# Encoder step: the convolution in three stretches instead of five, the sample's inputs in one tile with the last prompt inputs

## The chip, the core and the metric

The kernel runs on one core of one Trainium2 chip. The metric is the device time of one execution in microseconds (us). The kernel before takes 1810.93 us, the median of 3 runs (1809.39 to 1812.55). About 0.2% is what a measurement of this kernel can tell from no change.

## What is computed

One step of a streaming encoder of depth 1, for a prompt of 1024 tokens and a sample of 64 tokens that share the weights; both are kept side by side as 1088 columns. After a norm, one projection feeds four mixers: a convolution module, forgetting attention (fox), a gated recurrence (hgrn) and stick-breaking attention (sb), 256 channels each. Their outputs go through `w_out`; then come memory cross-attention, a squared-ReLU MLP and a final norm. The change touches the convolution module, here with the end of the layer that uses it:

```python
def _conv_module(a, g, hist, w, bias, ln_g, ln_b):
    u = a * sigmoid(g)
    ext = concatenate([hist, u], axis=1)         # hist: 30 rows before the first token
    y = depthwise_conv(ext, w)                   # 31 taps per channel
    yf = y + bias
    yn = layer_norm(yf, ln_g, ln_b)              # over the 256 channels
    return silu(yn), ext[:, -30:]
...
    x = x + concat([conv_o, fox_o, hg_o, sb_o]) @ w_out
```

The prompt's `hist` is zero, the sample's is the input `cache_conv`. The last 30 rows of `ext` of each are outputs (`conv_p`, `conv_s`).

## The kernel before, in words

**Layout.** Channels lie on the 128 partitions, tokens along the free dimension, columns 0 to 1023 the prompt, 1024 to 1087 the sample. Matrix products are made of three float32 passes (high and low parts): each weight tile of 512 KB is fetched on SP's queue (L179, tile `wr`, two buffers), copied to its high part on ACT (`wh`, L74) and subtracted to its low part on DVE (`wl`, L171), each with two buffers.

**Lanes.** The mixers are written as four generators that a loop (L980) advances by a virtual time: projections (`lane_projections`), attention, convolution and hgrn. What a generator yields is its estimate of the time of the piece just recorded. Every lane has a priority; the framework's scheduler then orders the instructions of each engine by priority and readiness. Projections come first, then attention, hgrn and convolution, and products on TensorE (`products`) behind these. The last thing the projection lane does is `memory_kv` (L371): 16 weight tiles of `w_mk` and `w_mv` ("the kv tiles"); each ends with a copy `mkvT` and a copy `mnat` on ACT. After the lanes, with a still later priority (PR_END), comes the rest.

**The convolution** (`lane_conv`, L740) works on stretches of the sequence: 288, 288, 288 and 160 columns of the prompt, then the 64 of the sample. For a stretch and each of the two channel halves it reads the value and gate projections back from DRAM (`ga`, `gg`, L756 and L757), makes the sigmoid on ACT and DVE, writes the product into `ext` (L759) behind the 30 columns of history, and runs 31 taps on DVE, each one instruction over the whole stretch (L764 for the first, L767 for thirty). Then comes the layer norm over channels, which lie on partitions: two sums on TensorE through a matrix of ones (`pme`, `pva`), the square root's reciprocal by `rstd_chain` (L140), scale and shift, another sigmoid, and a store to `mix_d` in DRAM (L799). Tiles with one buffer each, shared by tag: `c0`, `c1`, `c2` (288 columns; inputs, gates, and the norm's three work tiles), `ce0`, `ce1` (318; `ext`, then the squares), `cy0`, `cy1` (288; the results `y`).

**After the lanes** `mix_d` is read back: for columns 0 to 511 ("group 0", tile `mix`, L1000), and for 512 to 1087 ("group 1", tile `aq`, L1000 through `split_mix` at L1186). Each tile is split into high and low parts (`ap`). `dense_add` (L1072) multiplies by `w_out`: eight weight tiles for group 0 (tile `pa`, 512 columns), then eight for group 1 (320 and 256 columns), and adds each product to the residual `xt` (L1083), which L1159 loads. Group 1 multiplies slots 2 to 7 of the mixers first and the convolution's slots 0 and 1 last (`MIX`, L1189). Between the groups, `rms_stats` and `rms_apply` (L1041, L1063) make the norm of group 0: squares (L1038), a sum `pr` on TensorE, eight normed tiles (L1059) and their splits. Memory attention follows with `pq`.

Of the kernel before, what the change touches and what calls it, by code (L numbers as in the profile page):

```python
# [8 lines left out]
F32 = mybir.dt.float32  # L9
# [3 lines left out]
AF = mybir.ActivationFunctionType  # L13
# [4 lines left out]
P = 128  # L18
# [34 lines left out]
def kernel(ctx: ExitStack, tc: tile.TileContext, *args):  # L53
# [666 lines left out]

    HW = CW - 1
    CN = 288

    def ct_(name, tag, n=CN):
        return hc.tile([P, n], F32, name=name, tag=tag)
# [14 lines left out]
    def lane_conv():  # L740
        tails = [None, None]
        for t0, n in [(t, min(CN, SP - t)) for t in range(0, SP, CN)] + [(SP, SS)]:
            last = t0 + n >= SP
            ys, exts = [], []
            for ct in range(2):
                yield Need(ct)
                yield Need(2 + ct)
                ext = ct_(f"ext{ct}", f"ce{ct}", CN + HW)
                if t0 == SP:
                    V.tensor_copy(out=ext[:, :HW], in_=hT[:, ct])  # L750
                elif t0 == 0:
                    V.memset(ext[:, :HW], 0.0)
                else:
                    V.tensor_copy(out=ext[:, :HW], in_=tails[ct])
                ga, gg, sg = ct_("ga", "c0"), ct_("gg", "c1"), ct_("sg", "c2")
                nc.sync.dma_start(out=ga[:, :n], in_=pj_d[ct][:, t0:t0 + n])  # L756
                nc.sync.dma_start(out=gg[:, :n], in_=pj_d[2 + ct][:, t0:t0 + n])  # L757
                sigmoid(sg[:, :n], gg[:, :n])
                V.tensor_tensor(out=ext[:, HW:HW + n], in0=ga[:, :n], in1=sg[:, :n], op=ALU.mult)  # L759
                if not last:  # L760
# [5 lines left out]
                for j in range(1, CW):  # L766
                    V.scalar_tensor_tensor(out=y[:, :n], in0=ext[:, j:j + n], scalar=cwT[:, ct, j:j + 1], in1=y[:, :n],  # L767
                                           op0=ALU.mult, op1=ALU.add)
                    if j % 6 == 5:
                        yield 0.3 + n / 130.0  # L770
                ys.append(y[:, :n])
                exts.append(ext)
            if last:
                ps = ps_cv.tile([P, G], F32, name="pco", tag="cv")
                for ct in range(2):
                    nc.tensor.transpose(ps[:HW, ct * P:(ct + 1) * P], exts[ct][:, n:n + HW], ident)
                ot = ct_("cvo", "c0")
                V.tensor_copy(out=ot[:HW, :G], in_=ps[:HW])
                nc.sync.dma_start(out=(conv_s if t0 == SP else conv_p)[0, 0], in_=ot[:HW, :G])
            pm = ps_cv.tile([P, 512], F32, name="pme", tag="cv")  # L780
            for ct in range(2):
                mm(pm[:, :n], ones, ys[ct], ct == 0, ct == 1)
            sq = [ct_(f"sq{ct}", f"ce{ct}", CN + HW)[:, :n] for ct in range(2)]
            for ct in range(2):
                V.scalar_tensor_tensor(out=ys[ct], in0=pm[:, :n], scalar=-1.0 / G, in1=ys[ct],
                                       op0=ALU.mult, op1=ALU.add)
                act(sq[ct], ys[ct], AF.Square)
            pv2 = ps_cv.tile([P, 512], F32, name="pva", tag="cv")
            for ct in range(2):
                mm(pv2[:, :n], ones, sq[ct], ct == 0, ct == 1)  # L790
            r = rstd_chain(hc, n, pv2[:, :n], ("c0", "c1", "c2"), scale=1.0 / G)
            for ct in range(2):
                V.tensor_tensor(out=ys[ct], in0=ys[ct], in1=r, op=ALU.mult)
                V.tensor_scalar(out=ys[ct], in0=ys[ct], scalar1=cvec[:, 1, ct:ct + 1], scalar2=cvec[:, 2, ct:ct + 1],
                                op0=ALU.mult, op1=ALU.add)
                sg = ct_("sg2", "c2")[:, :n]
                sigmoid(sg, ys[ct])
                V.tensor_tensor(out=ys[ct], in0=ys[ct], in1=sg, op=ALU.mult)
                nc.sync.dma_start(out=mix_d[ct][:, t0:t0 + n], in_=ys[ct])  # L799
                yield 0.5 + n / 150.0  # L800
# [688 lines left out]
```

## Time and profile before

| | |
|---|---|
| median of 3 runs | 1810.93 us (1809.39 to 1812.55) |
| the profiled execution | 1812.65 us |
| its span, first to last instruction | 1810.6 us |
| busy in the span: PE, DVE, ACT, POOL | 96%, 66%, 44%, 5% |
| mean granted TensorE clock | 0.982 of 2.4 GHz |
| last kv product ends, first `pa` starts | 671.2 and 673.6 us |
| `w_out` group 0, first `pa` to last add | 673.6 to 729.6 us |
| `w_out` group 1, to its last product | 729.6 to 791.2 us |

The engines are PE (TensorE), DVE (VectorE), ACT (ScalarE), POOL (GpSimd) and SP, which issues nearly all transfers. Every engine runs its own instructions in the order in which they stand. A busy PE is not necessarily a PE at its full rate, so its time is read from a stage's length beside the rate of an undisturbed tile. PEclk is the granted clock as a share of 2.4 GHz.

### The profile page before, as it was taken

The page shows a single profiled execution, that of the slowest core. Times are in us where ns is not written, and L with a number is a line of the kernel's source. Part 1 is how long each engine was busy: PE and PEld are TensorE (multiplying, and loading weights), DVE is VectorE, ACT ScalarE, POOL GpSimd, SP SyncE. Part 2 cuts the span into 40 slices and gives each one's busy share as a digit, 9 for nine tenths or more (in the row PEclk, how much of TensorE's full clock was granted, in tenths as well). Part 3 has the DMA queues.
Part 4 walks back from the last instruction along what each step waited for, and adds up shares of the span by engine and source line. Part 5 has one row for each costly group of instructions (what it writes and reads, how often), then busy time and mean ns, then how long its engine had stood idle before and what let it go on. Part 6 is the DMA issues. An engine that isn't in the chain of part 4 may idle for free.

```text
span 1810.6 us, 29643 instructions
## 1 busy us (share of the span) xinstructions
PE 1731.0 (96%) x11454; PEld 1516.8 (84%) x11467; DVE 1199.6 (66%) x2362; ACT 794.2 (44%) x1619; POOL 96.9 (5%) x201
## 2 busy tenths in 40 slices
PE   7999999999999998899999959999999999999997
PEld 5877757778877877898899949999999999999987
DVE  6455778979887887856777696555555544444435
ACT  6464566455537843535556443434334312222113
POOL 3011202000220200000000000000000000000000
PEclk9999999999999999999999979999999999999999
DMA  7221212231223456422432322333334833222112
GB/s 243 83 77 37 64 46 75 69 82 60 84 89 98 139 159 214 119 85 63 142 104 72 95 85 95 98 104 104 116 105 133 317 97 97 96 90 66 47 35 100
DMA packets 227596, 184.87 MB, mean 102 GB/s; under 512 B 16510, under 2 KB 196415, under 8 KB 227455
## 3 DMA queue, kind: packets, MB, share of 16 engines
q1 hardware_dynamic: 227199, 182.96, 32.5%
q8 instruction: 90, 1.47, 0.4%
q14 instruction: 51, 0.42, 0.1%
q0 software_dynamic: 256, 0.01, 0.1%
HBM read 132.45 MB, written 50.44 MB: 101 GB/s over the span
## 4 chain that ended last, share of the span: by engine, by line
PE 56%; DVE 4%; ACT 1%; DMA 1%; issue 1%; DVEq 0%; ACTq 0%
PE pz L71 24%; PE pw L71 16%; PE pa L71 8%; PE pq L71 5%; PE pmo L71 1%; PE pms L71 1%; DVE y L767 0%; PE pmt L1144 0%; DVE ap L171 0%; PE pz L1414 0%; DVE wl L171 0%; ACT wh L74 0%; DVE tm L1059 0%; DVE xt L1083 0%; DVE xt L1059 0%
## 5 line engine op out<-in xcount | busy, mean ns | idle before, releaser
L74 ACT ACTIVATE wh<-wr 128x1024 fp32r<-128x1024 f32 (+1 forms) x180 | 161.4, 905 | 426.4 <-PE pz L71 195.4
L171 DVE TENSOR_TENSOR wl<-wr,wh 128x1024 fp32r<-128x1024 f32 (+1 forms) x180 | 184.8, 1034 | 67.9 <-ACT wh L74 66.9
L71 PE MATMUL pw<-ap,wh 128*128 128x512 f32 x704 | 220.0, 394 | 1.3 <-ACT t L74 0.7
L71 PE MATMUL pa<-ap,wh 128*128 128x512 f32 (+2 forms) x768 | 192.1, 337 | 5.4 <-DVE xt L1083 3.3
L71 PE MATMUL pz<-ap,wh 128*128 128x288 f32 x960 | 192.5, 294 | 0.0
L71 PE MATMUL pm<-hx,wh 128*128 128x512 f32 (+1 forms) x640 | 178.4, 366 | 2.0 <-ACT wh L74 2.0
L71 PE MATMUL pm<-ap,wh 128*128 128x256 f32 (+1 forms) x768 | 164.9, 308 | 0.0
L71 PEld LDWEIGHTS pz<-ap,wh 128*128 128x128 f32 x960 | 156.7, 188 | 4.9 <-DVE ap L1309 0.4
L71 PEld LDWEIGHTS pa<-ap,wh 128*128 128x128 f32 x768 | 134.6, 194 | 17.7 <-DVE xt L1083 3.4
L71 PEld LDWEIGHTS pw<-ap,wh 128*128 128x128 f32 x704 | 127.8, 189 | 23.8 <-ACT t L74 1.2
L71 PE MATMUL pw<-ap,wl 128*128 128x512 f32 x352 | 138.2, 392 | 5.6 <-DVE wl L171 5.6
L71 PE MATMUL pz<-ap,wl 128*128 128x288 f32 x480 | 141.0, 294 | 0.0
L71 PE MATMUL pa<-ap,wl 128*128 128x512 f32 (+2 forms) x384 | 128.8, 337 | 2.8 <-DVE wl L171 2.8
L71 PEld LDWEIGHTS pm<-hx,wh 128*128 128x128 f32 x640 | 111.3, 192 | 21.8 <-ACT wh L74 2.6
L71 PEld LDWEIGHTS pm<-ap,wh 128*128 128x128 f32 x768 | 124.1, 192 | 5.2 <-issue 1.9
L767 DVE SCALAR_TENSOR_TENSOR y<-ext,cwT,y 128x288 f32<-128x288 f32 (+2 forms) x300 | 125.3, 443 | 3.1
L1309 DVE TENSOR_TENSOR xt<-xt,pz 128x576 f32<-128x576 f32 x56 | 42.2, 753 | 114.4 <-PE pz L71 107.9
L71 PE MATMUL pm<-ap,wl 128*128 128x256 f32 (+1 forms) x384 | 114.3, 298 | 0.0
L71 PE MATMUL pm<-hx,wl 128*128 128x512 f32 (+1 forms) x320 | 112.8, 353 | 0.2 <-DVE wl L171 0.2
L1309 DVE TENSOR_TENSOR xt<-xt,pw 128x512 f32<-128x512 f32 (+2 forms) x80 | 51.0, 638 | 70.0 <-PE pw L71 67.7
L71 PE MATMUL pq<-ap,wh 128*128 128x512 f32 (+2 forms) x384 | 93.1, 331 | 0.0
L74 ACT ACTIVATE sba<-sba 128x127 f32<-128x127 f32 (+8 forms) x102 | 68.1, 682 | 55.2 <-DVE sba L490 54.4
(371 smaller groups left out, 3647.4 us busy)
## 6 DMA issues: line engine op xcount, KB each, us to landing
wr<-in_w_up_dram SPq DMA_DIRECT2D x32, 512.0 KB
wr<-in_w_down_dram SPq DMA_DIRECT2D x32, 512.0 KB
wr<-in_w_in_dram SPq DMA_DIRECT2D x24, 512.0 KB
hid_d<-ap SPq DMA_DIRECT2D x32, 288.0 KB
aq<-hid_d SPq DMA_DIRECT2D x32, 288.0 KB
wr<-in_w_out_dram SPq DMA_DIRECT2D x16, 512.0 KB
wr<-in_w_mq_dram SPq DMA_DIRECT2D x16, 512.0 KB
wr<-in_w_mo_dram SPq DMA_DIRECT2D x32, 256.0 KB
```

The costliest lines, as they stand in the source:

```text
L71: nc.tensor.matmul(out, lhsT=lhsT, rhs=rhs, start=start, stop=stop, **kw)
L74: nc.scalar.activation(out=out, in_=in_, func=func, **kw)
L171: V.tensor_tensor(out=lo, in0=src, in1=hi.bitcast(F32), op=ALU.subtract)
L767: V.scalar_tensor_tensor(out=y[:, :n], in0=ext[:, j:j + n], scalar=cwT[:, ct, j:j + 1], in1=y[:, :n], op0=ALU.mult, op1=ALU.add)
L1309: eng.tensor_tensor(out=out, in0=a, in1=b, op=ALU.add)
```

## The change

The convolution runs in three stretches: 352, 352, and 414 columns. The last one holds the prompt's last 320 columns, 30 columns in which the sample's history stands, and the 64 of the sample, in one `ext` tile; the 30 results over the seam mean nothing and are not stored. So there are 6 times 30 taps at L767 instead of 10 times 30. The value projection is loaded straight into `ext`, where the product is made in place. The gate input `gg` now shares the tag `cy` with `y`; the gate `sg`, the copy `cvo` and two of the norm's work tiles share `c0`; the squares, the norm's result and the last gate share `ce`. The layer norm runs over each stretch in two halves (176, 176; 176, 176; 207, 207). The lane yields after every third tap instead of every sixth, with other estimates.

```diff
     HW = CW - 1
-    CN = 288
-
-    def ct_(name, tag, n=CN):
+    CE = 320 + HW + SS
+
+    def ct_(name, tag, n=CE):
         return hc.tile([P, n], F32, name=name, tag=tag)
 
...
 
     def lane_conv():
         tails = [None, None]
-        for t0, n in [(t, min(CN, SP - t)) for t in range(0, SP, CN)] + [(SP, SS)]:
-            last = t0 + n >= SP
+        for t0, np_ in ((0, 352), (352, 352), (704, 320)):
+            last = t0 + np_ == SP
+            n, nt = (CE, np_ + SS) if last else (np_, np_)
             ys, exts = [], []
             for ct in range(2):
                 yield Need(ct)
                 yield Need(2 + ct)
-                ext = ct_(f"ext{ct}", f"ce{ct}", CN + HW)
-                if t0 == SP:
-                    V.tensor_copy(out=ext[:, :HW], in_=hT[:, ct])
-                elif t0 == 0:
+                ext = ct_(f"ext{ct}", f"ce{ct}", CE + HW)
+                if t0 == 0:
                     V.memset(ext[:, :HW], 0.0)
                 else:
                     V.tensor_copy(out=ext[:, :HW], in_=tails[ct])
-                ga, gg, sg = ct_("ga", "c0"), ct_("gg", "c1"), ct_("sg", "c2")
-                nc.sync.dma_start(out=ga[:, :n], in_=pj_d[ct][:, t0:t0 + n])
-                nc.sync.dma_start(out=gg[:, :n], in_=pj_d[2 + ct][:, t0:t0 + n])
-                sigmoid(sg[:, :n], gg[:, :n])
-                V.tensor_tensor(out=ext[:, HW:HW + n], in0=ga[:, :n], in1=sg[:, :n], op=ALU.mult)
-                if not last:
+                nc.sync.dma_start(out=ext[:, HW:HW + np_], in_=pj_d[ct][:, t0:t0 + np_])
+                if last:
+                    V.tensor_copy(out=ext[:, HW + np_:CE - SS + HW], in_=hT[:, ct])
+                    nc.sync.dma_start(out=ext[:, CE - SS + HW:], in_=pj_d[ct][:, SP:T])
+                gg, sg = ct_("gg", f"cy{ct}"), ct_("sg", "c0")
+                nc.sync.dma_start(out=gg[:, :nt], in_=pj_d[2 + ct][:, t0:t0 + nt])
+                sigmoid(sg[:, :nt], gg[:, :nt])
+                V.tensor_tensor(out=ext[:, HW:HW + np_], in0=ext[:, HW:HW + np_], in1=sg[:, :np_], op=ALU.mult)
+                if last:
+                    V.tensor_tensor(out=ext[:, CE - SS + HW:], in0=ext[:, CE - SS + HW:], in1=sg[:, np_:nt], op=ALU.mult)
+                else:
                     tails[ct] = hc.tile([P, HW], F32, name=f"tl{ct}", tag=f"tl{ct}", bufs=2)
                     V.tensor_copy(out=tails[ct], in_=ext[:, n:n + HW])
                 y = ct_(f"y{ct}", f"cy{ct}")
...
                 for j in range(1, CW):
                     V.scalar_tensor_tensor(out=y[:, :n], in0=ext[:, j:j + n], scalar=cwT[:, ct, j:j + 1], in1=y[:, :n],
                                            op0=ALU.mult, op1=ALU.add)
-                    if j % 6 == 5:
-                        yield 0.3 + n / 130.0
+                    if j % 3 == 2:
+                        yield 0.15 + n / 300.0
                 ys.append(y[:, :n])
                 exts.append(ext)
             if last:
-                ps = ps_cv.tile([P, G], F32, name="pco", tag="cv")
+                for at, dst in ((np_, conv_p), (CE, conv_s)):
+                    ps = ps_cv.tile([P, G], F32, name="pco", tag="cv")
+                    for ct in range(2):
+                        nc.tensor.transpose(ps[:HW, ct * P:(ct + 1) * P], exts[ct][:, at:at + HW], ident)
+                    ot = ct_("cvo", "c0")
+                    V.tensor_copy(out=ot[:HW, :G], in_=ps[:HW])
+                    nc.sync.dma_start(out=dst[0, 0], in_=ot[:HW, :G])
+            rs = ct_("rs", "c0").rearrange("p (j n) -> p j n", j=2)
+            sqs = [ct_(f"sq{ct}", f"ce{ct}", CE + HW) for ct in range(2)]
+            for p0, pn in ((0, n // 2), (n // 2, n - n // 2)):
+                yp = [y[:, p0:p0 + pn] for y in ys]
+                sq = [s[:, p0:p0 + pn] for s in sqs]
+                pm = ps_cv.tile([P, 512], F32, name="pme", tag="cv")
                 for ct in range(2):
-                    nc.tensor.transpose(ps[:HW, ct * P:(ct + 1) * P], exts[ct][:, n:n + HW], ident)
-                ot = ct_("cvo", "c0")
-                V.tensor_copy(out=ot[:HW, :G], in_=ps[:HW])
-                nc.sync.dma_start(out=(conv_s if t0 == SP else conv_p)[0, 0], in_=ot[:HW, :G])
-            pm = ps_cv.tile([P, 512], F32, name="pme", tag="cv")
-            for ct in range(2):
-                mm(pm[:, :n], ones, ys[ct], ct == 0, ct == 1)
-            sq = [ct_(f"sq{ct}", f"ce{ct}", CN + HW)[:, :n] for ct in range(2)]
-            for ct in range(2):
-                V.scalar_tensor_tensor(out=ys[ct], in0=pm[:, :n], scalar=-1.0 / G, in1=ys[ct],
-                                       op0=ALU.mult, op1=ALU.add)
-                act(sq[ct], ys[ct], AF.Square)
-            pv2 = ps_cv.tile([P, 512], F32, name="pva", tag="cv")
-            for ct in range(2):
-                mm(pv2[:, :n], ones, sq[ct], ct == 0, ct == 1)
-            r = rstd_chain(hc, n, pv2[:, :n], ("c0", "c1", "c2"), scale=1.0 / G)
-            for ct in range(2):
-                V.tensor_tensor(out=ys[ct], in0=ys[ct], in1=r, op=ALU.mult)
-                V.tensor_scalar(out=ys[ct], in0=ys[ct], scalar1=cvec[:, 1, ct:ct + 1], scalar2=cvec[:, 2, ct:ct + 1],
-                                op0=ALU.mult, op1=ALU.add)
-                sg = ct_("sg2", "c2")[:, :n]
-                sigmoid(sg, ys[ct])
-                V.tensor_tensor(out=ys[ct], in0=ys[ct], in1=sg, op=ALU.mult)
-                nc.sync.dma_start(out=mix_d[ct][:, t0:t0 + n], in_=ys[ct])
-                yield 0.5 + n / 150.0
+                    mm(pm[:, :pn], ones, yp[ct], ct == 0, ct == 1)
+                for ct in range(2):
+                    V.scalar_tensor_tensor(out=yp[ct], in0=pm[:, :pn], scalar=-1.0 / G, in1=yp[ct],
+                                           op0=ALU.mult, op1=ALU.add)
+                    act(sq[ct], yp[ct], AF.Square)
+                pv2 = ps_cv.tile([P, 512], F32, name="pva", tag="cv")
+                for ct in range(2):
+                    mm(pv2[:, :pn], ones, sq[ct], ct == 0, ct == 1)
+                v, r, t = rs[:, 0], sq[0], rs[:, 1]
+                rstd_chain(None, pn, pv2[:, :pn], "xxx", scale=1.0 / G, out=r, tiles=(v, t))
+                for ct in range(2):
+                    V.tensor_tensor(out=yp[ct], in0=yp[ct], in1=r, op=ALU.mult)
+                    V.tensor_scalar(out=yp[ct], in0=yp[ct], scalar1=cvec[:, 1, ct:ct + 1],
+                                    scalar2=cvec[:, 2, ct:ct + 1], op0=ALU.mult, op1=ALU.add)
+                for ct in range(2):
+                    sigmoid(sq[ct], yp[ct])
+                    V.tensor_tensor(out=yp[ct], in0=yp[ct], in1=sq[ct], op=ALU.mult)
+                    if not last or p0 == 0:
+                        nc.sync.dma_start(out=mix_d[ct][:, t0 + p0:t0 + p0 + pn], in_=yp[ct])
+                    else:
+                        nc.sync.dma_start(out=mix_d[ct][:, t0 + p0:SP], in_=ys[ct][:, p0:np_])
+                        nc.sync.dma_start(out=mix_d[ct][:, SP:T], in_=ys[ct][:, CE - SS:])
+                    yield 0.5 + pn / 150.0
```

How the instructions stand, at three places. First DVE around the weight splits for the last tiles of `w_out` group 0, before (`y` are taps of the sample, `cvo` the outputs `conv_s`):

```order
L767 SCALAR_TENSOR_TENSOR y_5512<-ext_5499,cwT,y_5512 128x64
L778 COPY cvo<-pco 30x256
L767 SCALAR_TENSOR_TENSOR y_5512<-ext_5499,cwT,y_5512 128x64
L1083 TENSOR_TENSOR xt<-xt,pa 128x512
L767 SCALAR_TENSOR_TENSOR y_5512<-ext_5499,cwT,y_5512 128x64
L171 TENSOR_TENSOR wl<-wr,wh 128x1024
L767 SCALAR_TENSOR_TENSOR y_5512<-ext_5499,cwT,y_5512 128x64
L171 TENSOR_TENSOR wl<-wr,wh 128x1024
L767 SCALAR_TENSOR_TENSOR y_5512<-ext_5499,cwT,y_5512 128x64 x9
```

And the change, DVE at the last two gates of the convolution (L166, L810; L1099 is the add that was L1083):

```order
L806 TENSOR_SCALAR y_4791<-y_4791,cvec 128x207
L171 TENSOR_TENSOR wl<-wr,wh 128x1024
L166 SCALAR_TENSOR_TENSOR sq_5100<-y_4422,sq_5100 128x207
L166 SCALAR_TENSOR_TENSOR sq_5101<-y_4791,sq_5101 128x207
L810 TENSOR_TENSOR y_4422<-y_4422,sq_5100 128x207
L810 TENSOR_TENSOR y_4791<-y_4791,sq_5101 128x207
L171 TENSOR_TENSOR ap<-mix,ap 128x512 x2
L171 TENSOR_TENSOR wl<-wr,wh 128x1024
L1099 TENSOR_TENSOR xt<-xt,pa 128x512
L171 TENSOR_TENSOR ap<-aq,ap 128x576 x2
```

Before, most of the sample's taps stand behind the fifth of group 0's eight adds, and two weight splits behind them; now the last instruction of the convolution stands ahead of the first add.

Second SP's queue, where the convolution's last results are stored. Before:

```order
L757 DMA gg<-pj_d 128x64
L756 DMA ga<-pj_d 128x64
L179 DMA wr<-in_w_out_dram 128x8x128
L1159 DMA xt<-xT_d 128x576 x5
L779 DMA out_dram<-cvo 30x256
L179 DMA wr<-in_w_out_dram 128x8x128 x3
L799 DMA mix_d<-y_5467 128x64
L1000 DMA aq<-mix_d 128x576
L799 DMA mix_d<-y_5512 128x64
L179 DMA wr<-in_w_out_dram 128x8x128
```

The change:

```order
L179 DMA wr<-in_w_out_dram 128x8x128
L814 DMA mix_d<-y_4422 128x113
L815 DMA mix_d<-y_4422 128x64
L814 DMA mix_d<-y_4791 128x113
L815 DMA mix_d<-y_4791 128x64
L1175 DMA xt<-xT_d 128x512 x2
L1016 DMA aq<-mix_d 128x576 x8
L1175 DMA xt<-xT_d 128x512 x2
L179 DMA wr<-in_w_out_dram 128x8x128
```

Before, the last two loads of mixer slots (`aq`) stand each behind a store of the sample's results, after four of the weight fetches shown here; now the four last stores stand in front of all eight `aq` loads and of the residual's first loads (`xt`).

Third ACT at the end of the kv tiles (`wr` here are the first tiles of `w_out`). Before:

```order
L74 ACTIVATE wh<-wr 128x1024
L74 ACTIVATE mkvT<-pm 128x256
L74 ACTIVATE mnat<-pn 128x256
L74 ACTIVATE wh<-wr 128x1024
L74 ACTIVATE mkvT<-pm 128x256
L74 ACTIVATE mnat<-pn 128x256
L74 ACTIVATE ap<-mix 128x512 x2
L74 ACTIVATE wh<-wr 128x1024
```

The change (`sq` holds the norm's squares and the last gate):

```order
L74 ACTIVATE mkvT<-pm 128x256
L74 ACTIVATE sq_5100<-y_4422 128x207
L74 ACTIVATE sq_5101<-y_4791 128x207
L74 ACTIVATE mnat<-pn 128x256
L74 ACTIVATE sq_5100<-sq_5100 128x207
L74 ACTIVATE sq_5101<-sq_5101 128x207
L74 ACTIVATE sq_5100<-sq_5100 128x207
L74 ACTIVATE sq_5101<-sq_5101 128x207
L74 ACTIVATE sq_5100<-sq_5100 128x207
L74 ACTIVATE sq_5101<-sq_5101 128x207
L74 ACTIVATE ap<-mix 128x512 x2
L74 ACTIVATE wh<-wr 128x1024
```

The gates of the last half-stretch now stand between the last copies of the kv tiles and the splits of `mix`, on which the seventh and eighth slot of group 0 rest.

## Rows read from the trace of the kernel before

**Rows 1.** Page, busy us of each engine over the span.

```profile
PE 1731.0 (96%) x11454; PEld 1516.8 (84%) x11467; DVE 1199.6 (66%) x2362; ACT 794.2 (44%) x1619; POOL 96.9 (5%) x201
```

**Rows 2.** Windows of 10 us: busy PE, PEld, DVE, ACT, POOL; PEclk, DMA share, GB/s.

```profile
670.00:680.00 10.00, 8.00 (x33) 6.35 (x33) 9.33 (x22) 2.97 (x5) 0.00 (x0) 0.83 0.85 244
...
710.00:720.00 10.00, 5.88 (x17) 4.02 (x16) 9.57 (x33) 0.94 (x1) 0.00 (x0) 0.73 0.29 84
...
760.00:770.00 10.00, 7.41 (x31) 6.95 (x32) 7.00 (x11) 1.27 (x2) 0.00 (x0) 0.66 0.46 131
...
780.00:790.00 10.00, 10.00 (x77) 10.00 (x77) 4.61 (x7) 1.63 (x2) 0.00 (x0) 1.00 0.35 104
```

**Rows 3.** Windows, same columns: w_out group 0, then group 1.

```profile
673.60:729.60 56.00, 51.45 (x210) 40.91 (x211) 44.53 (x132) 19.61 (x44) 0.00 (x0) 0.91 0.66 204
729.60:791.20 61.60, 56.12 (x387) 54.09 (x386) 41.83 (x65) 26.74 (x44) 0.00 (x0) 0.94 0.36 105
```

**Rows 4.** Timeline of DVE: adds of the w_out products (start, length).

```profile
692.72 0.69 DVE L1083 TENSOR_TENSOR xt<-xt,pa 128x512 f32<-128x512 f32 x1
...
698.16 0.69 DVE L1083 TENSOR_TENSOR xt<-xt,pa 128x512 f32<-128x512 f32 x1
...
781.93 0.49 DVE L1083 TENSOR_TENSOR xt<-xt,pa 128x320 f32<-128x320 f32 x1 [0.61 <-PE pa L71]
...
788.33 0.49 DVE L1083 TENSOR_TENSOR xt<-xt,pa 128x320 f32<-128x320 f32 x1 [0.61 <-PE pa L71]
```

**Rows 5.** Timeline of DVE: the sample's taps, weight splits behind them, last gate.

```profile
706.18 7.14 DVE L767 SCALAR_TENSOR_TENSOR y<-ext,cwT,y 128x64 f32<-128x64 f32 x36
713.24 0.40 DVE L778 COPY cvo<-pco 30x256 f32<-30x256 f32 x1
...
714.56 1.20 DVE L171 TENSOR_TENSOR wl<-wr,wh 128x1024 fp32r<-128x1024 f32 x1
...
715.89 1.21 DVE L171 TENSOR_TENSOR wl<-wr,wh 128x1024 fp32r<-128x1024 f32 x1
...
732.39 0.22 DVE L798 TENSOR_TENSOR y<-y,sg 128x64 f32<-128x64 f32 x1 [0.32 <-ACT sg L74]
```

**Rows 6.** Timeline of PE: waits at the w_out products.

```profile
711.00 0.73 PE L71 MATMUL pa<-ap,wh 128*128 128x512 f32 x2 [0.47 <-ACT wh L74]
...
713.70 0.43 PE L71 MATMUL pme<-y,ones 128*128 128x64 f32 x2 [1.97 <-DVE cvo L778]
...
715.82 0.80 PE L71 MATMUL pa<-ap,wl 128*128 128x512 f32 x1 [1.69 <-DVE wl L171]
...
739.17 0.53 PE L71 MATMUL pa<-ap,wh 128*128 128x320 f32 x2 [1.03 <-ACT ap L74]
```

**Rows 7.** Chain in order of time, 640 to 800: start, length, what.

```profile
698.09 2.38 DMA mix_d<-y
...
700.73 2.82 DMA gg<-pj_d
...
734.13 4.28 DMA aq<-mix_d
```

**Rows 8.** Timeline of DVE in group 1: first normed tiles, two weight splits.

```profile
751.20 2.07 DVE L1059 SCALAR_TENSOR_TENSOR tm<-xt,g_mem,tm 128x512 f32<-128x512 f32 x3
...
762.38 2.35 DVE L171 TENSOR_TENSOR wl<-wr,wh 128x1024 fp32r<-128x1024 f32 x2
```

**Rows 9.** Groups of DVE by form: weight splits, taps by width.

```profile
L171 DVE TENSOR_TENSOR wl<-wr,wh 128x1024 fp32r<-128x1024 f32 x116 | 142.1, 1225 | 65.2 <-ACT wh L74 65.0
...
L767 DVE SCALAR_TENSOR_TENSOR y<-ext,cwT,y 128x288 f32<-128x288 f32 x180 | 89.8, 519 | 1.7
...
L767 DVE SCALAR_TENSOR_TENSOR y<-ext,cwT,y 128x160 f32<-128x160 f32 x60 | 21.7, 381 | 0.7
...
L767 DVE SCALAR_TENSOR_TENSOR y<-ext,cwT,y 128x64 f32<-128x64 f32 x60 | 13.9, 278 | 0.6
```

**Rows 10.** Waits of PE between 280 and 673: us, times, longest.

```profile
PE pme L71 <- DVE y L767: 3.0, 1, 3.0
```

## The prediction

> **What bounds the kernel now.** I read the busy engines first, then the chain that ended last, windows along it, and the timelines of PE and DVE where a window shows PE short. Over the span PE is busy 96% and DVE 66% [rows 1]. So work that is taken off DVE is worth nothing by itself; it is worth time only where PE stands behind DVE. One such place belongs to the convolution: the two groups of `w_out` products, 673.6 to 791.2 us. An undisturbed tile takes 698.16 - 692.72 = 5.44 us in group 0 and 788.33 - 781.93 = 6.40 us in group 1, by the starts of equal adds [rows 4], with PE full and at 2.4 GHz in such a window, 780 to 790 [rows 2]. Eight and eight of these make 43.5 and 51.2 us. The groups took 56.0 and 61.6 us [rows 3]. So 12.5 and 10.4 us are lost, 22.9 us in all.
>
> Where they went: in group 0, DVE runs the sample's taps (36 of them in one run of 7.14 us), and two weight splits start only at 714.56 and 715.89 [rows 5]. PE waits 0.47, 1.97 and 1.69 us for ACT's copy, DVE's `cvo` and a split [rows 6], and the granted clock from 710 to 720 is 0.73, a part of it at 1.2 GHz [rows 2]. The last gate runs at 732.39 [rows 5], its store and the load of the eighth slot follow, 4.28 us from 734.13 on the chain [rows 7], and PE waits 1.03 us more for that slot's split at 739.17 [rows 6]. Then come the norm of group 0 and two weight splits at its end, from 762.38 [rows 8]; from 760 to 770 PE is busy 7.41 of 10 us, at a clock of 0.66 [rows 2].
>
> **The change part by part.**
>
> *Taps.* 300 instructions become 180. The durations are 519, 381 and 278 ns at 288, 160 and 64 columns [rows 9]; between 64 and 288 the slope is (519 - 278) / 224 = 1.08 ns a column, so I estimate 588 ns at 352 and 655 ns at 414. 120 x 0.588 + 60 x 0.655 = 109.9 us, against 89.8 + 21.7 + 13.9 = 125.4 us [rows 9]: 15.5 us less on DVE. Before 673.6 this lies beside PE's products, and I give it nothing there. Without that cover, with DVE the bound, it would be 15.5 us.
>
> *Place.* All taps, both half norms and all four last stores now stand ahead of the first add of group 0, in DVE's order and SP's. So DVE has only splits, adds and squares during group 0, and both convolution slots of group 1 are loaded with the six others.
> - Group 0: eight tiles, 43.5 us. The low clock at its start stays, from 670 to 680 10 x (1 - 0.83) = 1.7 us [rows 2], since PE also stands still for the last kv copies before. I add 1.0 us for transposes and sums that still run there. 46.2 instead of 56.0: **-9.8 us**. The waits for `cvo`, the split and ACT go; what is late next is the norm of group 0.
> - Group 1: eight tiles, 51.2 us. The wait for the eighth slot goes. The squares of group 0 are done during group 0 now, so its statistics start right behind the last add, some 10 us earlier against the tiles. But eight normed tiles and their splits still pass through DVE ahead of the fourth weight split. I keep a quarter of the 10.4 us, 2.6 us: 53.8 instead of 61.6, **-7.8 us**. Bounds: all of it stays (0), none (-10.4).
>
> *The kv tiles before.* Here the change adds. The second half norm and its gates stand between the last kv copies and the splits of `mix` on ACT and DVE, in-order queues. A late sum holds ACT's square, behind it the high parts of the next weights, and PE behind those. The trace has one such case, PE held for 3.0 us by a sum `pme` that waited for the last tap [rows 10]. I take one more of these, **+3.0 us**; the bounds are 0 (all of it beside products) and three of them, 9.0 us, since the last stretch has two halves and the middle one two. On SP, the four stores now stand in front of the residual's first loads, where six other loads stood between; PSUM has three buffers for `pa`, so an add that is 1 or 2 us late holds nothing.
>
> *Halves, shared tiles, shorter yields.* Six norms of half a stretch replace five of a whole; there are more instructions on ACT and the same columns, beside products: 0. That `gg` shares its tile with `y` makes its load wait for the store of the stretch before: 0 here, as the lane is a filler with two stretches of projections and kv products to hide in; its price is the second rival's.
>
> *Sum* against the profiled execution, 1812.65 us (its span is 1810.6, so 2.05 lies around it): 1812.65 - 9.8 - 7.8 + 3.0 = 1798.05. **I forecast 1798 us.** The profiled execution is 1.7 us above the median of 1810.93, so against that the forecast is 12.9 us, 0.7% faster. A measurement of this kernel can tell about 0.2%, 3.6 us.
>
> A rule to weigh at the longer taps. DVE's splits come 65.2 us late in all by the trace, and for 65.0 of these DVE stands idle for ACT's copy [rows 9]; so a split seldom finds a tap in its way, and I add nothing for taps of 0.655 us. The Trainium skill, Perfetto Trace Analysis, section Optimizing Scalar/DVE Operations, says the contrary of this change's direction: where such an engine is not saturated but makes bubbles on others, breaking instructions up may let work finish sooner. By it each of the 16 kv splits would wait up to 0.655 - 0.381 = 0.27 us longer, half of that on average, 2.2 us in all, and the sum would be 1800.2; no run here shows that yet.
>
> **The rivals.**
>
> 1. *Group 1 keeps its gap.* The stall at 760 is then not the convolution's but that of the norm of group 0, whose eight tiles and splits on DVE [rows 8] simply move with the stage. For it: at 760 the convolution is long over. Against: its squares waited behind the sample's last gates. 1812.65 - 9.8 + 3.0 = 1805.9 us. Chance 0.14.
>
> 2. *Slower: the lane ends late.* A stretch's load of `gg` may go only once the store of the stretch before has landed. The chain shows both halves of that round trip, 2.38 us for a store `mix_d` and 2.82 us for a load `gg` [rows 7]; two stretch boundaries and two channel halves make up to 4 x 5.2 = 20.8 us. If the last half norm so ends some 16 us behind the last kv product, ACT's and DVE's splits of `mix`, and SP's loads of the residual behind the four stores, hold group 0 for that long, and all that was won in both groups (17.6 us) is spent; below 16 us it is not. At the full 20.8 us: 1812.65 - 17.6 + 20.8 + 1.7 for a restart at the low clock = 1817.6 us. Against: two of the round trips can run beside each other, and the lane has about 100 us of kv and attention products to catch up in. Chance 0.17, of which 0.13 over 0.2% slower, 0.04 within. The Trainium skill, DMA: Bandwidth & Descriptors, section Rules for kernel authors, speaks for this rival: issue a transfer early and wait for it late, so that its fixed cost overlaps; the shared tile does the opposite.
>
> 3. *More: DVE's relief also helps before 673.* DVE loses 15.5 us there and PE has waits on it, 3.0 us of them at one sum [rows 10]; half of the 15.5 would make 1798 - 7.8 = 1790 us. Against: PE is busy 96% [rows 1]. Chance 0.11.
>
> 4. *The order is not what the edit intends*: that the sample's part still runs beside group 0. The order of the built program excludes it: no convolution instruction stands behind the first add. Chance 0.
>
> **How the numbers follow.** The forecast has 0.58: 1794 to 1803, by the bounds of the kv term and of group 1. Rival 1 is at the edge of what can be told (1807.3 us): 0.10 faster, 0.04 same. So faster 0.58 + 0.10 + 0.11 = 0.79, same 0.04 + 0.04 = 0.08, slower 0.13. The range from 1788 to 1811 takes in the forecast, rivals 1 and 3 and the milder part of rival 2; left out is its worse part and little else.
>
> **What would show it.** In the profile after: adds of group 0 every 5.4 us throughout, group 0 in about 46 us and group 1 in about 54; no window below a clock of 0.9 between the second tile of group 0 and `pq`; taps of about 0.59 and 0.65 us, 180 of them, all over before the first add. Rival 1: group 1 at 61 us. Rival 2: PE idle for over 10 us before `pa`, for ACT's or DVE's `ap` or the add; last store of the convolution far behind the last kv product. Rival 3: the first `pa` starts clearly before 673. I am wrong if `w_out` is no shorter, or if what it loses turns up ahead of it.

## The result and the profile after

The change takes 1795.91 us, the median of 4 runs (1791.5 to 1796.39), against 1810.76 us for the kernel before beside it: a ratio of 0.9909, with a 95% interval from 0.9894 to 0.9923, so some 15 us or 0.9% faster. The forecast was 1798 us. The profiled execution takes 1796.39 us, with a span of 1794.7 us.

The page's busy times, beside [rows 1]: DVE is busy 20 us less, PE 9 us less.

```profile
PE 1721.9 (96%) x11463; PEld 1511.7 (84%) x11475; DVE 1179.9 (66%) x2242; ACT 793.2 (44%) x1615; POOL 103.2 (6%) x201
```

The two groups of `w_out` products as windows (columns as in [rows 3]; cut at the first `pa`, the first product of 320 columns and the end of the last product; before, the cut between the groups lies at the last add, 0.2 us behind that first product), and under them three windows of 10 us:

```profile
672.21:717.47 45.26, 45.26 (x192) 37.27 (x193) 26.66 (x38) 21.14 (x34) 0.00 (x0) 0.96 0.88 280
717.47:774.20 56.73, 54.21 (x388) 53.20 (x387) 35.06 (x53) 19.54 (x28) 0.00 (x0) 0.97 0.30 90
...
670.00:680.00 10.00, 8.23 (x29) 6.47 (x30) 4.36 (x9) 5.77 (x14) 0.00 (x0) 0.83 0.91 260
...
710.00:720.00 10.00, 10.00 (x52) 8.71 (x51) 6.70 (x9) 5.70 (x8) 0.00 (x0) 1.00 0.66 192
...
730.00:740.00 10.00, 7.84 (x54) 7.58 (x54) 10.00 (x18) 4.67 (x7) 0.00 (x0) 0.91 0.18 52
```

Group 0 went from 56.0 to 45.3 us, and PE shows no pause in it; the stall from 710 to 720 of [rows 2] is gone. Group 1 went from 61.6 to 56.7 us, and a stall is left at 730 to 740. The first `pa` starts 1.4 us earlier (672.2 for 673.6), and what follows group 1 takes 1.1 us more (1794.7 - 774.2 = 1020.5 for 1810.6 - 791.2 = 1019.4). So -10.7 - 4.9 - 1.4 + 1.1 = -15.9 us, the difference of the two spans.

The taps on DVE by form (compare [rows 9]), and DVE's timeline at the convolution's last gates and at adds of group 0 (L1099, before L1083):

```profile
L773 DVE SCALAR_TENSOR_TENSOR y<-ext,cwT,y 128x352 f32<-128x352 f32 x120 | 68.3, 586 | 1.4
...
L773 DVE SCALAR_TENSOR_TENSOR y<-ext,cwT,y 128x414 f32<-128x414 f32 x60 | 38.2, 648 | 0.2
```

```profile
673.80 0.66 DVE L810 TENSOR_TENSOR y<-y,sq 128x207 f32<-128x207 f32 x2 [0.16 <-ACT sq L74]
...
701.35 0.69 DVE L1099 TENSOR_TENSOR xt<-xt,pa 128x512 f32<-128x512 f32 x1 [2.70 <-PE pa L71]
...
706.79 0.69 DVE L1099 TENSOR_TENSOR xt<-xt,pa 128x512 f32<-128x512 f32 x1 [2.69 <-PE pa L71]
```

The last two gates run from 673.8 to 674.5, some 58 us earlier than the last one of [rows 5] at 732.4, and equal adds stand 5.44 us apart, as in the undisturbed pair of [rows 4].

### The profile page after: what moved, and what is told of

It reads as the page before. It is cut to its first block, busy times and chain, and to the rows that moved or that the text cites. A ratio compares the mean times of both kernels' runs of the same rounds, so it can differ in the third digit from the quotient of the medians.

```text
span 1794.7 us, 29493 instructions
## 1 busy us (share of the span) xinstructions
PE 1721.9 (96%) x11463; PEld 1511.7 (84%) x11475; DVE 1179.9 (66%) x2242; ACT 793.2 (44%) x1615; POOL 103.2 (6%) x201
## 4 chain that ended last, share of the span: by engine, by line
PE 57%; DVE 5%; DMA 2%; ACT 1%; issue 1%; POOL 0%; SPq 0%; DVEq 0%; ACTq 0%; POOLq 0%
PE pz L71 23%; PE pw L71 16%; PE pa L71 8%; PE pq L71 5%; PE pmo L71 1%; PE pms L71 1%; DMA kr<-mkT_d 1%; PE pm L71 1%; DVE wl L171 1%; DVE ap L171 0%; PE pmt L1160 0%; PE pz L1430 0%; DVE tm L1075 0%; ACT wh L74 0%; DMA mix_d<-ho 0%
## 5 line engine op out<-in xcount | busy, mean ns | idle before, releaser
L171 DVE TENSOR_TENSOR wl<-wr,wh 128x1024 fp32r<-128x1024 f32 (+1 forms) x180 | 184.6, 1032 | 70.8 <-ACT wh L74 69.8
L71 PE MATMUL pa<-ap,wh 128*128 128x256 f32 (+2 forms) x768 | 187.6, 332 | 2.6 <-DVE xt L1099 2.2
L773 DVE SCALAR_TENSOR_TENSOR y<-ext,cwT,y 128x352 f32<-128x352 f32 (+1 forms) x180 | 106.4, 607 | 1.6
```

The lines of the kernel that those rows point to most:

```text
L71: nc.tensor.matmul(out, lhsT=lhsT, rhs=rhs, start=start, stop=stop, **kw)
L171: V.tensor_tensor(out=lo, in0=src, in1=hi.bitcast(F32), op=ALU.subtract)
```

## The experiments

Eleven kernels ran. The table is taken from their profiles, one execution each (that of experiment 2 took 1819.7 us and that of 7 1799.9, each 5.7 above its median): stretches of the convolution, busy time of the taps on DVE, end of the last tap and of the last gate, first `pa`, length of the two groups (all us), and the median time with its ratio to the kernel before on the same chip.

| kernel | stretches | taps | last tap | last gate | first `pa` | group 0 | group 1 | median | ratio (95%) |
|---|---|---|---|---|---|---|---|---|---|
| before | 5 | 125.4 | 720 | 733 | 673.6 | 56.0 | 61.6 | 1810.8 | 1 |
| the change | 3 | 106.5 | 643 | 674 | 672.2 | 45.3 | 56.7 | 1795.9 | 0.9909 (0.9894 to 0.9923) |
| 1 merged, four stretches | 4 | 115.9 | 697 | 716 | 676.8 | 68.8 | 54.9 | 1825.5 | 1.0084 (1.0069 to 1.0099) |
| 2 narrow taps | 3 | 120.7 | 707 | 724 | 677.9 | 63.0 | 57.3 | 1814.0 | 1.0026 (1.0012 to 1.004) |
| 3 before, few sample taps | 5 | 112 | 706 | 718 | 672.7 | 48.0 | 63.4 | 1805.1 | 0.9966 (0.9954 to 0.9977) |
| 4 spread norm | 3 | 106.5 | 642 | 674 | 671.6 | 44.8 | 52.7 | 1793.2 | 0.9911 (0.989 to 0.9932) |
| 5 before, convolution first | 5 | 126.0 | 645 | 658 | 652.2 | 79.6 | 61.4 | 1815.0 | 1.0016 (0.9999 to 1.0033) |
| 6 sample apart | 4 | 113.6 | 686 | 699 | 670.4 | 49.4 | 57.4 | 1799.6 | 0.9936 (0.9914 to 0.9958) |
| 7 whole norm | 3 | 105.9 | 646 | 676 | 678.3 | 45.1 | 55.5 | 1794.2 | 0.9906 (0.9875 to 0.9937) |
| 8 whole norm, spread | 3 | 106.0 | 638 | 668 | 670.3 | 44.5 | 52.5 | 1789.9 | 0.9888 (0.9859 to 0.9916) |
| 9 before, few prompt taps | 5 | 102.2 | 683 | 696 | 672.4 | 46.2 | 55.2 | 1799.8 | 0.9942 (0.9925 to 0.996) |
| 10 as 1, `cvo` on ACT | 4 | 115.8 | 701 | 719 | 680.1 | 70.0 | 54.9 | 1827.9 | 1.0095 (1.008 to 1.011) |
| 11 as 1, own gate tiles | 4 | 115.6 | 694 | 712 | 675.8 | 55.5 | 56.6 | 1809.4 | 0.999 (0.9974 to 1.0005) |

The first theory, A, was the forecast's: the sample's part no longer stands among the `w_out` products in the instruction order. Its rival B was that the saved DVE time is what counts.

**1. The sample merged, but four stretches** (against the change; `CE` and the tile widths follow).

```diff
-        for t0, np_ in ((0, 352), (352, 352), (704, 320)):
+        for t0, np_ in ((0, 288), (288, 288), (576, 288), (864, 160)):
```

> The sample merged into the last prompt stretch, but stretches of 288 as before (288, 288, 288, 254): 240 taps, by the widths of before 180 x 0.519 + 60 x 0.48 = 122 us on DVE, only 3 us less than before (125.4). Theory A (place: the gain comes because the sample's taps, norm and stores no longer stand among the w_out products): nearly the whole gain stays, group 0 46 to 48 us, total 1796 to 1801. Theory B (relief: the gain comes from the DVE time that fewer, longer taps save, 15.5 us in the change): only a fifth of it is left, total 1806 to 1809.

It took 1825.5 us: slower than before, which neither theory had. All its taps stand ahead of the first add in DVE's order, as in the change, but they run late. DVE's block of taps, and PE's waits at the first `w_out` tile:

```profile
672.30 19.77 DVE L773 SCALAR_TENSOR_TENSOR y<-ext,cwT,y 128x254 f32<-128x254 f32 x50
```

```profile
676.82 1.19 PE L71 MATMUL pa<-ap,wh 128*128 128x512 f32 x4 [0.52 <-ACT mnat L74]
692.43 0.61 PE L783 MATMUL pco<-ident,ext 128*30 128x128 f32 x2 [14.42 <-DVE cvo L785]
695.15 0.80 PE L71 MATMUL pme<-y,ones 128*128 128x127 f32 x2 [2.11 <-DVE cvo L785]
```

This is what the second rival of the prediction described: the lane is late, and the splits of `w_out` wait behind it on in-order queues. So a place in the instruction order is not a place in time, and theory A falls as I had stated it.

**2. Taps of two stretches cut in two** (against the change).

```diff
-                    V.scalar_tensor_tensor(out=y[:, :n], ...
+                    for q0, qn in (((0, 176), (176, 176)) if not last else ((0, n),)):
+                        V.scalar_tensor_tensor(out=y[:, q0:q0 + qn], ...
```

> The change, but each tap of the first two stretches cut into two instructions of 176 columns (300 taps, as many as before): 240 x 0.40 + 60 x 0.65 = 135 us on DVE, 10 us more than before and 28 more than the change; same stretches, loads, norms and stores. Theory A: the sample's part still ends at the start of group 0, total 1796 to 1803, unless the lane's end slips behind the last kv product by more than a few us. Theory B: the whole gain and more is gone, 1811 or above.

1814.0 us. The edit only cuts the taps, and with 14.2 us more of them on DVE (120.7 for 106.5) the last gate came at 724, 50 us later. The pieces, by form:

```profile
L774 DVE SCALAR_TENSOR_TENSOR y<-ext,cwT,y 128x176 f32<-128x176 f32 x240 | 81.8, 402 | 0.1
```

B's number, but by its own measure B was out: 120.7 us are still fewer than the 125.4 of before. Nor are the 50 us the taps' own: the two pauses between the stretches, from the last of these taps to the next, took 51.6 us (391.9 to 443.5) and 78.1 us (535.6 to 613.7), and in the change 38.6 us (379.2 to 417.8) and 33.8 us (485.7 to 519.5).

**3. The kernel before with 2 of the sample's 60 taps** (58 are left out).

```diff
                 for j in range(1, CW):
+                    if t0 < SP or j == 1:
                         V.scalar_tensor_tensor(...
```

> The kernel before with 2 of the sample's 60 taps at L767 (58 left out, 16 us of DVE); its loads, norm, gates and stores stay where they are. If the taps held DVE's splits in group 0 (as I read it): the stall at 710 to 720 goes, group 0 about 47 us, and the last slot is there in time, total 1796 to 1802. If it is the latency of the sample's norm, store and load that holds group 0 and 1: group 0 stays above 52 us, total 1806 or more.

1805.1 us, between the two ranges. The taps did hold group 0: it takes 48.0 us without them. But group 1 stayed at 63.4 us, so the 4.9 us that it won in the change are not the sample's taps'. PE's timeline there:

```profile
730.01 1.12 PE L71 MATMUL pr<-aq,ones 128*128 128x512 f32 x2
747.84 0.80 PE L71 MATMUL pa<-ap,wh 128*128 128x256 f32 x2 [5.24 <-DVE xt L1084]
```

The norm of group 0 (`pr`) starts 9.4 us into group 1 (its start is 720.7), and PE then waits 5.24 us for an add.

**4. The normed tiles of group 0 spread over group 1's weight tiles** (against the change).

```diff
-        h2 = rms_apply(0, g_mem, rms_stats(0, ps2, "sc"), 0)
-        dense_add(1, w_out, 0, KD, mix[1], ps1, lambda m: load_x(1, m), order=MIX)
+        rr0 = rms_stats(0, ps2, "sc")
+        h2 = [pair(0) for _ in range(KD)]
+        def ahead1(m):
+            load_x(1, m)
+            for k in ((), (), (0,), (1,), (2,), (3,), (4, 5), (6, 7))[m]:
+                hf = normed(0, k, g_mem, rr0, 0, 512)
+                split(h2[k][0][:, :512], h2[k][1][:, :512], hf[:, :512])
+        dense_add(1, w_out, 0, KD, mix[1], ps1, ahead1, order=MIX)
```

> The change, with the eight normed tiles of group 0 (and their splits) recorded one or two per weight tile of group 1, not all ahead of it, so that they no longer stand ahead of the adds on DVE. If what group 1 still loses (56.7 us against 51.2) is PE's 2.15 us wait for the add behind the normed tiles and the low clock after it: group 1 52 to 53.5 us, total 1791 to 1793. If it is the sum and the square root's chain itself: no change, 1795 to 1797.

Group 1 took 52.7 us, as expected:

```profile
716.40:769.10 52.70, 52.48 (x388) 51.74 (x387) 34.55 (x52) 19.31 (x28) 0.00 (x0) 1.00 0.32 96
```

In the change, DVE ran five pairs of a normed tile and its split (L1075, L171) in a row from 730.7 on, and the adds that free PSUM stood behind them; PE waited 2.15 us for one (row below, in the last section). In this kernel no such wait is left. The gain of 4 us shows in the stage and not in the total: the median of 1793.2 us is 2.7 below the change's, but the ratio to the kernel before is 0.9911 here and 0.9909 there.

The first two runs gave a third theory, C: what counts is when the lane ends against the end of the kv tiles, and that is set by its turnarounds (the pauses between stretches, from a last tap through norm, stores and loads to the next first tap, 20 to 58 us each before) as much as by its taps.

**5. The kernel before, convolution ahead of hgrn.**

```diff
-PR_PROJ, PR_ATT, PR_HGRN, PR_CONV, PR_MM, PR_END = ...
+PR_PROJ, PR_ATT, PR_CONV, PR_HGRN, PR_MM, PR_END = ...
```

> The kernel before with one edit: the convolution's lane ranks ahead of hgrn's (the two priorities swapped). All 300 taps, five stretches and 125 us of taps on DVE stay. Theory C (what counts is when the lane's last gate falls against the end of the kv tiles, 733 against 673 us before, 674 against 669 in the change; that end is set by the five or three turnarounds from a stretch's last tap to the next one's first, 20 to 58 us each, as much as by the taps): the last gate falls before 673, group 0 takes 45 to 47 us, total 1796 to 1802, provided hgrn does not become the late lane in its place (then 1806 to 1815, with PE or ACT waiting for ho). Theory B (DVE time saved): as before, 1808 to 1812.

1815.0 us. The convolution ended at 658, 6 us behind the first `pa` (652.2), where it ended 59 us behind it before, with all its taps and stretches; but hgrn became the late lane, and its products and waits now lie in group 0. PE's waits for it:

```profile
670.33 0.87 PE L849 MATMUL phhvn<-ident,hv 128*128 128x128 f32 x3 [3.58 <-DVE ho L960]
677.43 1.12 PE L71 MATMUL pz<-qz,ky 128*64 128x128 f32 x4 [6.22 <-POOL ky L873]
```

Its proviso came true, so it tells nothing between B and C: moved forward without being made less, this lane's work only made another lane late.

**6. The sample in a stretch of its own again** (against the change; the merged loads, product and stores go).

```diff
-        for t0, np_ in ((0, 352), (352, 352), (704, 320)):
+        for t0, np_ in ((0, 352), (352, 352), (704, 320), (SP, SS)):
```

> The change with the sample in a stretch of its own again: 352, 352, 320, 64, four stretches, 240 taps, about 120 us on DVE. Theory C: a fourth turnaround of 30 us puts the last gate at 700 to 715 and the sample's taps beside group 0, total 1803 to 1811; less than the 1825 us of the merged four stretches, since only 64-column taps stand ahead of the adds. Theory A (it is enough that the sample's taps stand ahead of the first add in DVE's order, as they do here too): 1796 to 1800.

1799.6 us, better than C expected and inside the range of A, which experiment 1 had already ruled out; the last gate, at 699, is 25 us later than in the change. The merging itself is worth some 4 us, and by the intervals perhaps nothing; most of the gain stays without it. In experiment 1 the last stretch's first gate product also ran at 666 to 667 us, and the taps that then stood ahead of the splits were 254 columns wide; here they are 64:

```profile
672.04 8.33 DVE L770 SCALAR_TENSOR_TENSOR y<-ext,cwT,y 128x64 f32<-128x64 f32 x42
```

**7 and 8. The norm over whole stretches**, alone and with the spread of experiment 4 (against the change).

```diff
-            for p0, pn in ((0, n // 2), (n // 2, n - n // 2)):
+            for p0, pn in ((0, n),):
...
-                v, r, t = rs[:, 0], sq[0], rs[:, 1]
+                v, r, t = rs, sq[0], sq[1]
```

> The change with each stretch's layer norm whole, not in two halves (the work tiles are the squares' own). From the first subtraction to the last gate the change takes 28, 24 and 29 us with halves; before took 17, 23, 47 and 15 with whole ones. Theory C: each turnaround 5 to 10 us shorter, last gate at 640 to 665; w_out is clean already, so the time hardly moves: 1793 to 1797. Rival (the halves let the taps' splits and sums through, whole ones hold ACT and PE): 1798 to 1803.

> The change with the whole norms of the run before this one and the normed tiles of group 0 spread over group 1's weight tiles (1793.2 us alone). If the two are independent: 1790 to 1793. If the earlier end of the lane has a worth of its own ahead of w_out: below 1789.

1794.2 and 1789.9 us. C's expectation of a last gate at 640 to 665 was missed: whole norms ended the lane at 676 and 668, for 674 with halves, and did not make the time worse. The halves are not what matters. The two edits together give the fastest kernel of the study, a ratio of 0.9888 to before; its interval overlaps the change's.

**9. The kernel before without 48 prompt taps** (8 of 30 in each 288-column stretch are left out).

```diff
                 for j in range(1, CW):
+                    if n < CN or j <= 22:
                         V.scalar_tensor_tensor(...
```

> The kernel before with 8 of the 30 taps left out in each of the three 288-column stretches: 48 x 0.519 = 25 us less on DVE, 100 us of taps, less than in the change (106). Five stretches and all turnarounds stay, and the sample's taps too. Theory B (DVE time): the lane ends 40 us or more earlier, as it ended 50 us later when 28 us were added; last gate before 695, total 1796 to 1802. Theory C1 (the number of turnarounds): the lane ends less than 25 us earlier, after 708, total 1803 to 1811.

1799.8 us, inside B's range, with five stretches and the sample's taps and norm all there; B's bounds for the lane, 40 us earlier and before 695, were missed by 3 and 1 us. The lane's last gate, and groups 0 and 1:

```profile
695.83 0.23 DVE L799 TENSOR_TENSOR y<-y,sg 128x64 f32<-128x64 f32 x1 [0.32 <-ACT sg L74]
```

```profile
672.39:718.61 46.22, 46.22 (x199) 37.89 (x200) 32.97 (x67) 22.13 (x40) 0.00 (x0) 0.96 0.87 275
718.61:773.82 55.21, 52.73 (x388) 51.73 (x387) 34.95 (x53) 19.51 (x28) 0.00 (x0) 1.00 0.32 94
```

DVE time taken off between 300 and 510 us, 23 us of it, ended the lane 37 us earlier and gave both groups nearly the lengths that they have in the change. It is not the number of turnarounds alone: C as put in this run's expectation falls. Yet five stretches with 102.2 us of taps end at 696, and three with 106.5 us at 674, so something beside the taps has a part, some 22 us of the lane's end. The fewer turnarounds are the likely cause; it is not shown, since the two kernels differ in tiles and loads too. Nor does the lane's end by itself order the kernels: it is 716 in experiment 1 and 733 before, and experiment 1 is 15 us slower than before.

**10. Experiment 1 with `pco` in one PSUM tile and the copies on ACT.**

```diff
-                    V.tensor_copy(out=ot[:HW, :G], in_=ps[:HW])
+                    act(ot[:HW, :G], ps[:HW, i], AF.Copy)
```

> The merged four stretches (1825.5 us), with both outputs' transposes in one PSUM tile and their copies cvo on ACT, so that PE's transposes no longer wait for a DVE copy behind 50 taps (14.4 us of PE's wait there). If that copy is the cause: total 1808 to 1813. If it only hides what comes next, the weight split and the splits of mix behind the same taps on DVE: PE waits for wl or ap instead, total 1820 to 1826.

1827.9 us: no better. The releaser that the timeline had named was not the cause; PE now waits for what stood next behind the same taps:

```profile
695.08 0.80 PE L71 MATMUL pme<-y,ones 128*128 128x127 f32 x2 [12.89 <-DVE y L773]
```

**11. Experiment 1 with own tiles for gate input and gate.**

```diff
-                gg, sg = ct_("gg", f"cy{ct}"), ct_("sg", "c0")
+                gg, sg = ct_("gg", "c1"), ct_("sg", "c2")
```

> The merged four stretches with the gate input in a tile of its own (not y's) and the gate in another, so that a stretch's gate load and sigmoid no longer wait for the stores and the norm of the one before. My second rival's price was 5.2 us for each store and load. If these round trips set the lane's pace: three turnarounds 5 to 10 us shorter each, the last taps start 15 to 25 us earlier than 667, total 1805 to 1815. If the ext load (which still shares with the squares) or DVE's other work sets it: 1820 to 1826.

1809.4 us, 16 us better than experiment 1, by two tiles, and as expected if the round trips set the pace: the three turnarounds, by the taps at L773, are 6.3, 3.5 and 5.7 us shorter. The last stretch's first product now runs at 646 rather than 667, so more than half of its taps pass before the kv tiles end; 26 stood in the block ahead of the splits, not 50:

```profile
669.43 10.32 DVE L773 SCALAR_TENSOR_TENSOR y<-ext,cwT,y 128x254 f32<-128x254 f32 x26
```

So the shared tiles of `gg` and `sg` do cost a lane its round trips, as the second rival said of `gg`. In the change itself it was not tried.

## Why the prediction was right, and where its steps were not

**The number** held: 1798.05 us against 1796.39 for the profiled execution. That it is so close is in part luck. The sum had three terms and nothing for all else, and their errors went both ways: group 0 won 0.9 us more than forecast and the stretch ahead of the first `pa` 4.4 us more, group 1 won 2.9 us less, and what follows group 1 lost 1.1 us that had no term.

- *Group 0*: forecast 46.2 us, measured 45.3. Right in size: the low clock at the start stayed (0.83 from 670 to 680), and no other stall did.
- *Group 1*: forecast 53.8, measured 56.7. I kept a quarter of the 10.4 us, 2.6; 5.5 stayed. The mis-sized part is DVE's normed tiles: I set them against the fourth weight split, but what they hold is the adds, and by them PSUM and PE (experiment 4 takes 4.0 us of it away). The trace of before has the same wait, PE's longest in this group, and I did not read it:

```profile
760.98 0.50 PE L71 MATMUL pa<-ap,wh 128*128 128x256 f32 x2 [2.79 <-DVE xt L1083]
```

  That group 1 gained at all was put down to the last slot and to squares behind the sample's gates. In experiment 3, with the last gate at 718, the norm's sum `pr` starts 9.4 us into group 1, which takes 63.4 us; in the change it starts 3.3 us into it (720.78 - 717.47), and PE's wait for the add is 2.15 us rather than 5.24:

```profile
720.78 1.12 PE L71 MATMUL pr<-aq,ones 128*128 128x512 f32 x2 [0.36 <-DVE aq L1054]
```

  That agrees with the step, but no run moved the gates alone, and in experiment 5, whose gates are over at 658, group 1 still takes 61.4 us.
- *The kv tiles*: forecast +3.0, measured -1.4 for all that lies ahead of the first `pa`, with one profile of each. Experiment 4, which differs from the change only behind that point, has its first `pa` 0.6 us earlier (671.6 for 672.2). I doubled the one hold of [rows 10]; it shrank instead, by the same view of the change:

```profile
PE pme L71 <- DVE y L773: 0.3, 1, 0.3
```

- *Taps*: forecast 588 and 655 ns, measured 586 and 648; 106.5 us for a forecast of 109.9. But the step "I give it nothing there" had the wrong reason behind a right number. I took the place from the instruction order and the saving as a side effect. Experiments 2 and 9 show that the taps' time on DVE moves the lane's end, and by more than itself: with 14 us more of it the lane ended 50 us later, with 23 us less 37 us earlier. Its worth is not paid where it is saved, between 300 and 510 us in experiment 9, but from 672 us on, at the first products that need the engine which the lane still occupies.
- *Place*: the sentence that all of the convolution stands ahead of the first add was true and carried the forecast, but it proves less than I thought. In experiment 1 the taps do so too, and the kernel is 15 us slower than before. The order tells what waits for what; only a trace tells whether the work in front is done by then.

**The rivals.** Rival 1 (group 1 stays at 61 us) and rival 3 (7.8 us won ahead of the first `pa`) did not come. Rival 2 did not come in the change, whose last gate at 673.8 is 2 us behind the first `pa`, but experiment 1 is that rival, 1825 us for its 1817.6. Its threshold, 16 us late, was too simple: experiment 6 ends its lane at 699, 29 us after the first `pa`, and loses some 4 us. The longest block of late taps on DVE ahead of the first splits orders these kernels: 8.3 us in experiment 6, 10.3 in 11, 19.8 in 1, with groups 0 of 49.4, 55.5 and 68.8 us. It is not all: the first split of `mix` runs at 680.8 in experiment 6 and at 680.4 in 11, and in 11 PE waits a further 3.1 and 2.1 us for `cvo`, whose copies stand among the taps.

**The edits costed at nothing.** The halves of the norm: right (experiment 7). The shorter yields: no run tries the old ones, so the 0 is not shown. The shared tile of `gg`: what it costs in the change is not shown; where the lane has no slack, `gg` and `sg` together cost 16 us (experiment 11).

**The two rules.** The Trainium skill, Perfetto Trace Analysis, section Optimizing Scalar/DVE Operations, says that breaking instructions up may let work finish sooner where the engine is not saturated but makes bubbles on others. No run here agrees: with the taps cut, experiment 2 is 18 us slower than the change, as 240 pieces keep DVE busy for 81.8 us and the 120 whole taps for 68.3. Nor does the cost of 2.2 us show that the prediction worked out by it for the longer taps: PE waits for no weight split between 280 and 673 us of the change, and its first `pa` came 1.4 us earlier. The Trainium skill, DMA: Bandwidth & Descriptors, section Rules for kernel authors, says to issue a transfer early and wait for it late; experiment 11 agrees, with 16 us.

**What stays open**: how the change's gain divides between fewer turnarounds and less DVE time. Both move the lane's end, and no run holds the one fixed while the other alone moves as far as in the change; experiment 2 lengthens the turnarounds by touching the taps alone. What makes a turnaround longer or shorter there was not looked into.

## What to carry to other kernels

A filler lane that runs beside a longer one is judged by when its last instruction ends against the stage that follows, and by what stands behind it, not by its busy time: before that moment its cost is hidden, and after it each microsecond on an in-order queue ahead of the next stage's first operands is paid, often with a slower clock on top. Time saved in such a lane is looked for at its end, far from where it was saved. An instruction order that has the lane in front is good only if the lane is done by then; where it is late, the same order is worse than one that lets the next stage pass.

## What was not expected of the hardware

PE's pause of 2.15 us in group 1 of the change costs more than its own length. The rows of PE's timeline behind it, and two undisturbed ones of the same shape further on:

```profile
737.58 0.51 PE L71 MATMUL pa<-ap,wh 128*128 128x256 f32 x2 [2.15 <-DVE xt L1099]
...
738.49 0.63 PE L71 MATMUL pa<-ap,wh 128*128 128x256 f32 x2
...
739.13 0.63 PE L71 MATMUL pa<-ap,wh 128*128 128x256 f32 x2
...
746.28 0.40 PE L71 MATMUL pa<-ap,wh 128*128 128x256 f32 x2
...
746.64 0.40 PE L71 MATMUL pa<-ap,wh 128*128 128x256 f32 x2
```

The first products run at full speed, then equal steps take 0.64 us instead of 0.36 until 741.5, at 1.2 GHz, the lower of the clock's two levels, and then it is over. Five steps of it cost 5 x 0.28 = 1.4 us more. The window behind the pause in the change, and then the pause and the window behind it in experiment 9, where the same add holds PE as long:

```profile
738.30:741.60 3.30, 3.30 (x18) 3.30 (x17) 2.36 (x4) 0.68 (x1) 0.00 (x0) 0.50 0.13 29
```

```profile
738.68 0.50 PE L71 MATMUL pa<-ap,wh 128*128 128x256 f32 x2 [2.15 <-DVE xt L1084]
...
739.40:742.70 3.30, 3.30 (x29) 3.30 (x28) 2.78 (x5) 1.60 (x2) 0.00 (x0) 1.00 0.10 30
```

So the clock does not always fall. In seven profiles this add holds PE for 2.14 to 2.16 us. The lower clock follows in the change and in experiments 2 and 11, and group 1 takes 56.7, 57.3 and 56.6 us; it does not in 1, 7, 9 and 10, and group 1 takes 54.9 to 55.5 us. What decides, no run shows. So 1 to 2 us of the difference between two of these kernels can be the clock's and not the edit's. Where PE waits 14.4 us at once, in experiment 1, the granted clock of group 0 is 0.83.
